# Gate matrices of an expert layer: one-hot tiles interleaved by two tokens instead of four

## The chip, the cores and the metric

The kernel runs on one core of one Trainium2 chip. The core has five engines that run side by side: TensorE (PE; its weight loads are listed apart as PEld), VectorE (DVE), ScalarE (ACT), GpSimd (POOL) and SyncE (SP, which here issues DMAs). The metric is the device time of one execution in microseconds.

## The reference

The program is two blocks of two layers each, on 256 tokens of width 1024. The change lies in the expert part (`peer`) of the first block, which runs once per layer:

```python
s1 = jnp.einsum("thd,hnd->thn", q1, k1); s2 = jnp.einsum("thd,hnd->thn", q2, k2)
v1, i1 = lax.top_k(s1, TOPK); v2, i2 = lax.top_k(s2, TOPK)       # TOPK 16, 128 keys, 8 heads
cand = (v1[..., :, None] + v2[..., None, :]).reshape(t, PEER_HEADS, TOPK * TOPK)
sv, ci = lax.top_k(cand, TOPK)
e1 = jnp.take_along_axis(i1, ci // TOPK, axis=-1); e2 = jnp.take_along_axis(i2, ci % TOPK, axis=-1)
experts = e1 * N_KEYS + e2                                       # one of 128 x 128
gates = jax.nn.softmax(sv, axis=-1)
hid = jax.nn.gelu(jnp.einsum("td,tkd->tk", xi, u_tab[ei]))
out = jnp.einsum("tk,tkd->td", gi * hid, v_tab[ei])
```

Each token picks 128 pairs (8 heads x 16) of a row key `e1` and a column key `e2`, each with a gate.

## The kernel before

The kernel doesn't gather experts. It computes the hidden values of all 128 x 128 experts for all tokens, multiplies them by a gate matrix that is zero for what wasn't picked, and multiplies by all of `v`. The result of the first two lies in `big`, 128 partitions x 128 x 256 tokens.

The expert rows (`peer`, lines 1109 to 1119): for each `j` of 128 one `gemm` (line 464) with 8 pieces of the width, three matmuls each, since every f32 matrix is split into a high and a low part: 24 matmuls of 128 x 256 into the PSUM tile `mm`. Weights come by DMA into `st` and are split by ScalarE (`wh`) and VectorE (`wl`) in line 381. After each `gemm`, `pump` lets a generator (`topk`) emit some of its instructions, and `hid` (line 1201) applies the gelu and, where the token's gate is there already, multiplies by it (line 1208).

The gates (`topk`, lines 1312 to 1346): after the top-k the tile `egt` holds, for each of 128 picks on the partitions and each token, the row key, the column key, and the gate as two f16 parts. For a block of 4 tokens VectorE makes four f16 tiles of 128 x 512 in one buffer `o` (two buffers, carved out of `x`, so that the trace calls them `x`): `o[:, 0]` and `o[:, 1]` are one where the index equals the row or the column key (line 1324), and `o[:, 2]` and `o[:, 3]` are `o[:, 1]` times the two gate parts (line 1326). Then TensorE makes each token's 128 x 128 gate matrix as two matmuls (line 1346, recorded as line 430, `g<-x`), with `o[:, 0]` as weights and `o[:, 2]`, `o[:, 3]` as the moving operand, for that token alone: 8 matmuls per block, 64 blocks per layer, two layers. VectorE (line 1335) and ScalarE (line 1337) write the gates into `big`.

Within a tile the index is the slow dimension and the token of the block the fast one: element `4 * i + t`. So VectorE's operands have runs of four, and a matmul for token `q` reads every fourth element, a step of 8 bytes. `iota4` is the index row repeated in that layout, cast once per layer (line 1074).

The order in which instructions stand on an engine is set when the program is built, by a list scheduler with a cost model; each engine then works in that order.

Of the kernel before, what the change touches and what calls it, by code (L numbers as in the profile page):

```python
# [12 lines left out]
F16 = mybir.dt.float16  # L13
# [6 lines left out]
P = 128  # L20
# [392 lines left out]
class Builder:  # L413
# [635 lines left out]
    def peer(self, l):  # L1049
        nc, tc = self.nc, self.tc  # L1050
        with tc.tile_pool(name=f"pe{l}", bufs=1) as sp, tc.tile_pool(name=f"pew{l}", bufs=2) as wk, \
                tc.tile_pool(name=f"pep{l}", bufs=2, space=PSUM) as pp:
            big = self.t(sp, [P, P, T], tag="big")
            egt = self.t(sp, [P, 4, T], F16, tag="egt")
            self.big, self.egt = big, egt
            self.iota8 = self.t(sp, [P, 16, 8], F16, tag="iota8")
            self.iota4 = self.t(sp, [P, 4 * P], F16, tag="iota4")
            with tc.tile_pool(name=f"peh{l}", bufs=1) as hp:
                hi = self.t(hp, [P, KD, T], F32R, tag="hi")
                lo = self.t(hp, [P, KD, T], F32R, tag="lo")  # L1060
                flat = big.rearrange("p j t -> p (j t)")
                front = Carve(flat[:, :4096], 4096)
                tail = Carve(flat[:, J0 * T:], (P - J0) * T)
                pk = self.t(tail, [P, 2, 1024], tag="pk", bufs=1)
                for n in range(2):
                    nc.gpsimd.dma_start(pk[:, n], self.I["pk"][l, n])
                self.warm(pp, "g", WP[0], 2)
                ss = self.sumsq((self.t(self.psp, [P, 512], tag="pss", bufs=1) if FD & 1 else self.t(pp, [P, 512], tag="mm"))[:, :T])
                self.warm(pp, "g", WP[1], 2)
                r = self.rsq(ss, T, front, tag="nrm", bufs=1)  # L1070
                self.norm(self.x, lambda k: self.g(f"norm2_g{l}", k), None, hi, lo, front, r)
                with self.after(self.nins):
                    nc.vector.tensor_copy(self.iota8, self.iota[:, :16].unsqueeze(2).to_broadcast([P, 16, 8]))
                    nc.vector.tensor_copy(self.iota4.rearrange("p (i t) -> p i t", t=4),
                                          self.iota.unsqueeze(2).to_broadcast([P, P, 4]))
                nc.gpsimd.dma_start(self.xd[l], self.x)
                self.ohp = Carve(self.x.rearrange("p k t -> p (k t)"), KD * T)
                rhs = lambda k: (hi[:, k, :], lo[:, k, :])
                sc = [self.t(tail, [P, 16, P], tag="sc") for _ in range(2)]
                scp = None  # L1080
                pend = []

                def score(b, ps):
                    nonlocal scp
                    qt = self.t(front, [P, T], tag="qt")
                    nc.scalar.copy(qt, ps)
                    if b % 4 == 0:
                        scp = [self.t(pp, [P, 4, P], tag=f"sc{t}", bufs=1) for t in range(2)]
                    key = pk[:, b % 2, (b // 2) * P:(b // 2 + 1) * P]
                    for t in range(2):  # L1090
                        self.mm(scp[t][:, b % 4, :], qt[:, t * P:(t + 1) * P], key, start=True, stop=True)
                    if b % 4 == 3:
                        for t in range(2):
                            nc.scalar.copy(sc[t][:, b - 3:b + 1, :], scp[t])
                        self.scored = b + 1

                self.J, self.gtok, self.scored = 0, 0, 0
                self.tkdone = False
                self.bg.append(self.topk(l, sc, tail, wk, pp))
                for b in range(16):  # L1100
                    w = self.stream.get("wq", (l, b), 0, 1024)
                    ps = self.t(pp, [P, 512], tag="mm")[:, :T]
                    self.gemm(ps, w, KD, rhs)
                    self.pump(PUMP0)
                    if pend:
                        score(*pend.pop())
                    pend.append((b, ps))
                score(*pend.pop())
                for j in range(P):
                    if j == J0:  # L1110
                        while not self.tkdone:
                            self.pump(1)
                    w = self.stream.get("u", (l, j), 0, 1024)
                    ps = self.t(pp, [P, 512], tag="mm")[:, :T]
                    self.gemm(ps, w, KD, rhs)
                    self.pump(PUMP if j < J0 else PUMP2)
                    if pend:
                        self.hid(*pend.pop(), wk)
                    pend.append((j, ps))
                self.hid(*pend.pop(), wk)  # L1120
                self.drain()
# [3 lines left out]
            with tc.tile_pool(name=f"pev{l}", bufs=2) as vp:  # L1125
# [24 lines left out]
                for j in range(P):  # L1150
# [23 lines left out]
                    for gs in ((0,), (1,), (2,), (3,)) if last else ((0, 2), (1, 3)):  # L1174
                        a = gs[0] % 2
                        ts = slice(a * P, (a + 1) * P)
                        for q, wh, wl, vh, vl in W:
                            for w, vs in ((wh, (vh, vl)), (wl, (vh,))):
                                for g in gs:
                                    h = g // 2  # L1180
                                    for v in vs:
                                        self.mm(acc[g], w[:, q % 2, ts], v[:, h * 512:(h + 1) * 512],
                                                start=q == 0 and w is wh and v is vh,
                                                stop=q == P - 1 and w is wl)
# [28 lines left out]
    def topk(self, l, sc, tl, wk, pp):  # L1213
        nc, big, egt = self.nc, self.big, self.egt
# [21 lines left out]
        for t in range(2):  # L1236
# [22 lines left out]
            g = hk(eg[:, 2, :])  # L1259
# [45 lines left out]
            ps = self.t(pp, [P, 4, P], tag="sc0", bufs=1)  # L1305
# [6 lines left out]
        NB = T // 4  # L1312
        oh = {}
        gp = {}
        io = self.iota4.rearrange("p (i t) -> p i t", t=4)
        for b in range(NB + 2):
            if b < NB:
                o = self.t(self.ohp, [P, 4, 4 * P], F16, tag="oh", bufs=2)
                o = o.rearrange("p n (i t) -> p n i t", t=4)
                oh[b] = o  # L1320
                e = [egt[:, n, 4 * b:4 * b + 4].unsqueeze(1).to_broadcast([P, P, 4]) for n in range(4)]
                for n in range(4):
                    if n < 2:
                        nc.vector.tensor_tensor(o[:, n], io, e[n], op=OP.is_equal)
                    else:
                        nc.vector.tensor_tensor(o[:, n], o[:, 1], e[n], op=OP.mult)  # L1326
                    yield 330
            if b >= 2:
                ps = gp.pop(b - 2)
                t0 = 4 * (b - 2)  # L1330
                J = self.J
                pv = ps.rearrange("p t j -> p j t")
                if J > 0:
                    d = big[:, :J, t0:t0 + 4]
                    nc.vector.scalar_tensor_tensor(d, pv[:, :J, :], 1.0 / GS, d, op0=OP.mult, op1=OP.mult)
                if J < P:
                    nc.scalar.activation(big[:, J:, t0:t0 + 4], pv[:, J:, :], AF.Copy, scale=1.0 / GS)
                self.gtok = t0 + 4
                yield 450
            if 1 <= b <= NB:  # L1340
                o = oh.pop(b - 1)
                ps = self.t(pp, [P, 4, P], tag="g")
                gp[b - 1] = ps
                for q in range(4):
                    for n in range(2, 4):
                        self.mm(ps[:, q, :], o[:, 0, :, q], o[:, n, :, q], start=q == 0 and n == 2, stop=n == 3)

    def mods(self, l, qs, acc, pool):
        nc = self.nc
# [745 lines left out]
```

## Time and profile before

| what | us |
|---|---|
| median of 3 runs (lowest, highest) | 3112.36 (3111.44, 3113.1) |
| profiled execution: time, span | 3113.49, 3111.7 |
| PE busy | 3021.3 |
| DVE busy | 2226.6 |
| ACT busy | 1504.2 |
| POOL busy | 216.9 |

The span runs from the first to the last instruction; the rest of the profiled execution's time lies around it. A busy TensorE is not one at its peak: matmuls are pipelined, their recorded durations overlap, and the pace is read from the distance of their starts. Nearly all of TensorE's matmuls have one line, 430, since a helper records them; the tiles' names tell them apart.

### The profile page before, as it was taken

Reading aid. Unit: us, or ns where it says so; the run is one execution under the profiler, and the core shown is the slowest. Engines: PE = TensorE matmul, PEld = TensorE weight load, DVE = VectorE, ACT = ScalarE, POOL = GpSimd, SP = SyncE. Lnnn points to the kernel's source line nnn. Section 1 sums busy time; section 2 is a strip of 40 time slices with the busy share of each in tenths; the row PEclk is TensorE's granted clock in tenths of the full one; section 3 lists DMA queues with packets and bytes.
Section 4 is the critical chain, followed back from the end, with each engine's and each line's share of the span. In section 5 each row is a group of like instructions: output and inputs, shape, how many; then the busy total and the mean of one; then the engine's idle time right before and its main releaser. Section 6 shows DMA issues by size and latency. Waiting matters only on the chain. (4 is left out here: it accounts for less than half of the span.)

```text
span 3111.7 us, 50024 instructions
## 1 busy us (share of the span) xinstructions
PE 3021.3 (97%) x19130; PEld 2674.5 (86%) x19130; DVE 2226.6 (72%) x4322; ACT 1504.2 (48%) x2547; POOL 216.9 (7%) x262
## 2 busy tenths in 40 slices
PE   7999999999999889999999999998999999999999
PEld 7899999987887879999997788776688878977899
DVE  8789688789555969868869855667567773476554
ACT  7545444444444655444444444557532222377443
POOL 4200000000001720000000000100020001100100
PEclk8999999999999999999999999999999999999999
DMA  4455544578665445654458766521145553231455
GB/s 153 142 160 180 159 140 136 159 267 276 191 193 176 127 138 163 180 153 138 141 164 291 255 190 193 160 73 39 38 135 183 183 180 107 100 102 55 136 183 149
DMA packets 133599, 489.32 MB, mean 157 GB/s; under 512 B 15024, under 2 KB 15280, under 8 KB 132208
## 3 DMA queue, kind: packets, MB, share of 16 engines
q1 hardware_dynamic: 130608, 472.65, 49.2%
q0 software_dynamic: 2608, 13.44, 1.3%
q8 instruction: 150, 2.46, 0.3%
q14 instruction: 89, 0.73, 0.1%
q10 hardware_dynamic: 144, 0.05, 0.0%
HBM read 480.83 MB, written 5.24 MB: 156 GB/s over the span
## 5 line engine op out<-in xcount | busy, mean ns | idle before, releaser
L381 ACT CAST wh<-st 128x1024 fp32r<-128x1024 f32 (+1 forms) x797 | 832.6, 1046 | 1071.6 <-PE mm L430 657.8
L381 DVE TENSOR_TENSOR wl<-st,wh 128x1024 fp32r<-128x1024 f32 (+1 forms) x797 | 975.8, 1226 | 442.7 <-ACT wh L381 439.6
L430 PE MATMUL mm<-hi,wh 128*128 128x256 f32 (+1 forms) x3552 | 1086.9, 308 | 11.7 <-DVE hi L643 8.1
L430 PE MATMUL mm<-hi,wl 128*128 128x256 f32 (+1 forms) x3552 | 1065.7, 300 | 6.7 <-DVE wl L381 6.7
L430 PE MATMUL mm<-lo,wh 128*128 128x256 f32 (+1 forms) x3552 | 1066.8, 301 | 3.1 <-DVE lo L643 2.8
L430 PEld LDWEIGHTS mm<-hi,wh 128*128 128x128 f32 x3552 | 682.6, 193 | 46.6 <-issue 9.3
L430 PEld LDWEIGHTS mm<-lo,wh 128*128 128x128 f32 x3552 | 683.6, 192 | 29.4 <-DVE lo L643 6.8
L430 PEld LDWEIGHTS mm<-hi,wl 128*128 128x128 f32 x3552 | 682.5, 192 | 29.6 <-DVE wl L381 8.0
L430 PE MATMUL sc<-wl,wwh 128*128 128x512 f32 x496 | 195.2, 394 | 0.0
L430 PE MATMUL g<-wl,wwh 128*128 128x512 f32 x496 | 193.2, 389 | 0.0
L430 PE MATMUL g<-wh,wwl 128*128 128x512 f32 x496 | 193.1, 389 | 0.0
L430 PE MATMUL sc<-wh,wwl 128*128 128x512 f32 x496 | 193.1, 389 | 0.0
L430 PE MATMUL sc<-wh,wwh 128*128 128x512 f32 x496 | 192.3, 389 | 0.0
L430 PE MATMUL g<-wh,wwh 128*128 128x512 f32 x496 | 192.3, 389 | 0.0
L1326 DVE TENSOR_TENSOR x<-x,egt 128x512 f16<-128x512 f16 x256 | 107.3, 422 | 84.2 <-PE g L430 84.2
L1155 ACT CAST wwh<-big 128x512 fp32r<-128x512 f32 x124 | 77.2, 624 | 148.0 <-PE g L430 148.0
L430 PE MATMUL g<-x 128*128 128x128 f16 x1024 | 142.5, 296 | 0.0
L1394 DVE SCALAR_TENSOR_TENSOR sreg<-tl,silc,sreg 128x512 f32<-128x512 f32 x168 | 120.0, 747 | 7.3 <-DMA tl<-in_mod 6.9
L1394 DVE SCALAR_TENSOR_TENSOR sreg<-mb,silc,sreg 128x512 f32<-128x512 f32 x168 | 117.0, 747 | 8.7 <-DMA mb<-in_mod 8.4
L430 PE MATMUL mm<-fl,wh 128*128 128x256 f32 (+1 forms) x374 | 122.4, 327 | 0.0
L430 PE MATMUL mm<-fh,wh 128*128 128x256 f32 (+1 forms) x374 | 122.4, 327 | 0.0
L430 PE MATMUL mm<-fh,wl 128*128 128x256 f32 (+1 forms) x374 | 122.3, 327 | 0.0
(551 smaller groups left out, 4376.1 us busy)
## 6 DMA issues: line engine op xcount, KB each, us to landing
st<-in_u SPq DMA_DIRECT2D x256, 512.0 KB, 3.7
st<-in_v SPq DMA_DIRECT2D x256, 512.0 KB, 3.8
st<-in_fi SPq DMA_DIRECT2D x88, 512.0 KB, 3.4
st<-in_w SPq DMA_DIRECT2D x58, 512.0 KB, 3.7
tl<-in_mod SPq DMA_DIRECT2D x48, 512.0 KB, 4.9
mb<-in_mod SPq DMA_DIRECT2D x48, 512.0 KB, 4.3
st<-in_wq SPq DMA_DIRECT2D x32, 512.0 KB, 4.0
st<-in_fo SPq DMA_DIRECT2D x32, 512.0 KB, 3.7
```

The costliest lines, as they stand in the source:

```text
L381: self.last = [b.nc.scalar.copy(hi, t).ins, b.nc.vector.tensor_sub(lo, t, hi).ins]
L430: self.lastmm = self.nc.tensor.matmul(out, lhsT=a, rhs=b, start=start, stop=stop, skip_group_check=True).ins
L1155: nc.scalar.copy(wh, big[:, j:j + 2, :])
L1326: nc.vector.tensor_tensor(o[:, n], o[:, 1], e[n], op=OP.mult)
L1394: nc.vector.scalar_tensor_tensor(a, w[:, k % 2], s, a, op0=OP.mult, op1=OP.add)
```

## The change

The four tokens of a block are laid out as two groups of two: element `256 * g + 2 * i + t`. A matmul for token `q` now reads group `q // 2`, every second element: a step of 4 bytes, for the weights and the moving operand. VectorE's instructions keep their number and size, but the pattern of the operands changes: the key operand has runs of two that are repeated 128 times in each of two groups, and the index row (`iota2`, half as long) is repeated for the two groups. The cast that lays it out has 256 elements a partition in place of 512. On all five engines the instructions stand in the same order as before, one for one.

```diff
@@ peer
-            self.iota4 = self.t(sp, [P, 4 * P], F16, tag="iota4")
+            self.iota2 = self.t(sp, [P, 2 * P], F16, tag="iota2")
...
-                    nc.vector.tensor_copy(self.iota4.rearrange("p (i t) -> p i t", t=4),
-                                          self.iota.unsqueeze(2).to_broadcast([P, P, 4]))
+                    nc.vector.tensor_copy(self.iota2.rearrange("p (i t) -> p i t", t=2),
+                                          self.iota.unsqueeze(2).to_broadcast([P, P, 2]))
@@ topk
-        io = self.iota4.rearrange("p (i t) -> p i t", t=4)
+        io = self.iota2.rearrange("p (i t) -> p i t", t=2).unsqueeze(1).to_broadcast([P, 2, P, 2])
...
-                o = o.rearrange("p n (i t) -> p n i t", t=4)
+                o = o.rearrange("p n (g i t) -> p n g i t", g=2, t=2)
                 oh[b] = o
-                e = [egt[:, n, 4 * b:4 * b + 4].unsqueeze(1).to_broadcast([P, P, 4]) for n in range(4)]
+                e = [egt[:, n, 4 * b:4 * b + 4].rearrange("p (g t) -> p g t", g=2).unsqueeze(2)
+                     .to_broadcast([P, 2, P, 2]) for n in range(4)]
...
-                        self.mm(ps[:, q, :], o[:, 0, :, q], o[:, n, :, q], start=q == 0 and n == 2, stop=n == 3)
+                        self.mm(ps[:, q, :], o[:, 0, q // 2, :, q % 2], o[:, n, q // 2, :, q % 2],
+                                start=q == 0 and n == 2, stop=n == 3)
```

## Rows read from the trace of the kernel before

**Rows 1.** The page: busy time by engine, and the chain that ended last.

```profile
PE 3021.3 (97%) x19130; PEld 2674.5 (86%) x19130; DVE 2226.6 (72%) x4322; ACT 1504.2 (48%) x2547; POOL 216.9 (7%) x262
...
PE mm L430 22%; PE s L430 3%; PE o L430 1%; PE pt L1749 1%; PE pss L430 0%; PE ss L430 0%; DVE lo L643 0%; ACT wh L381 0%; PE pss L1362 0%; DVE mb L643 0%; DVE hi L643 0%; DMA mb<-in_mod 0%; DVE wl L381 0%; DMA st<-in_fi 0%; ACT at L1750 0%
```

**Rows 2.** Stretches: length, busy PE, PEld, DVE, ACT, POOL, clock, DMA share, GB/s.

```profile
372.00:548.00 176.00, 176.00 (x1478) 173.53 (x1477) 144.77 (x324) 80.23 (x185) 0.00 (x0) 1.00 0.46 138
...
586.00:630.00 44.00, 44.00 (x369) 44.00 (x368) 23.41 (x30) 20.74 (x31) 0.00 (x0) 1.00 0.62 181
...
1370.00:1546.00 176.00, 176.00 (x1477) 173.50 (x1476) 144.75 (x322) 80.26 (x185) 0.00 (x0) 1.00 0.46 138
...
525.00:548.00 23.00, 23.00 (x195) 22.68 (x194) 19.93 (x44) 10.13 (x25) 0.00 (x0) 1.00 0.47 137
555.40:563.00 7.60, 7.60 (x66) 7.54 (x64) 7.43 (x17) 3.56 (x10) 0.00 (x0) 1.00 0.45 140
```

**Rows 3.** Groups by shape, 372 to 548 us: busy, mean ns | idle before.

```profile
L430 PEld LDWEIGHTS mm<-hi,wh 128*128 128x128 f32 x368 | 71.0, 193 | 0.1
...
L1324 DVE TENSOR_TENSOR x<-iota,egt 128x512 f16<-128x512 f16 x93 | 38.9, 419 | 0.0
L1326 DVE TENSOR_TENSOR x<-x,egt 128x512 f16<-128x512 f16 x92 | 38.9, 422 | 31.2 <-PE g L430 31.2
L430 PEld LDWEIGHTS <-x 128*128 128x128 f16 x372 | 37.6, 118 | 2.4
```

**Rows 4.** Timeline, from 395 us: start, duration, engine, instruction.

```profile
395.04 1.10 PE L430 MATMUL g<-x 128*128 128x128 f16 x8
...
395.85 0.21 PEld L430 LDWEIGHTS mm<-hi,wh 128*128 128x128 f32 x1
395.90 0.37 PE L430 MATMUL mm<-hi,wh 128*128 128x256 f32 x1
...
398.85 1.12 PE L430 MATMUL g<-x 128*128 128x128 f16 x8
...
402.67 1.11 PE L430 MATMUL g<-x 128*128 128x128 f16 x8
```

**Rows 5.** Timeline of TensorE without gates: the first and the 25th matmul.

```profile
590.04 0.28 PE L430 MATMUL mm<-lo,wh 128*128 128x256 f32 x1
...
592.92 0.28 PE L430 MATMUL mm<-lo,wh 128*128 128x256 f32 x1
```

**Rows 6.** Timeline of bf16 matmuls in the attention of layer 0.

```profile
82.79 0.38 PE L430 MATMUL s<-kt,qz 128*128 128x256 f32 x1
...
83.12 0.22 PE L430 MATMUL s<-maskb,identb 128*128 128x128 bf16 x1
...
83.17 0.22 PE L430 MATMUL s<-cum,oh 128*128 128x128 bf16 x1
83.17 0.10 PEld L430 LDWEIGHTS <-identb 128*128 128x128 bf16 x1
83.23 0.22 PE L430 MATMUL s<-maskb,identb 128*128 128x128 bf16 x1
83.23 0.19 PEld L430 LDWEIGHTS s<-kt,qz 128*128 128x128 f32 x1
83.28 0.43 PE L430 MATMUL s<-kt,qz 128*128 128x256 f32 x1
```

**Rows 7.** Tile `g`: all gate matmuls, ns least/median/most, first and last start.

```profile
L430 PE MATMUL g<-x x1024: 282/297/302, 289.3 to 1577.6; 128*128 128x128 f16 x171
```

**Rows 8.** VectorE: groups of 280 to 340 us, then line 1156.

```profile
L1302 DVE TENSOR_TENSOR big<-big 128x1024 f16<-128x1024 f16 x2 | 1.4, 682 | 0.0
L1296 DVE TENSOR_TENSOR big<-big,iota 128x2048 f16<-128x2048 f16 x1 | 1.2, 1218 | 0.0
L1302 DVE TENSOR_TENSOR big<-big 128x512 f16<-128x512 f16 x2 | 0.8, 395 | 0.0
...
L1156 DVE TENSOR_TENSOR wwl<-big,wwh x124: 677/692/695, 638.5 to 1978.5; 128x512 fp32r<-128x512 f32 x124
```

## The prediction

> **What bounds the kernel now.** I read the page first. TensorE is busy for 97% of the span, VectorE for 72%, and the chain that ended last is made of TensorE's matmuls of line 430 for nearly all that it follows back [rows 1]. So the question for each stage is whether TensorE ever waits in it. I then took the stretches. The gate matmuls of a layer run in one stretch, spread between the hidden-layer matmuls of the expert rows: 372 to 548 us in layer 0 and 1370 to 1546 us in layer 1 hold most of them. [...] Grouped by shape, VectorE's only wait in the first stretch is 31.2 us, of `x` (line 1326) for the gate matmuls, 0.68 us in each of the 46 periods [rows 3]. VectorE waits for TensorE and not the other way, and a us taken off TensorE here is a us off the end, until VectorE's 0.68 us are used up.
>
> Then one period of the stretch in order of time. It holds one expert row of 24 matmuls of 256 columns, and one gate block of 8 matmuls of 128 columns. Blocks start at 395.04, 398.85 and 402.67 us, so a period is 3.82 us [rows 4]. The same 24 matmuls without gates take 2.88 us (from 590.04 to 592.92), 0.120 us each, at the same clock [rows 2, 5]. So a gate block costs 3.82 - 2.88 = 0.94 us, or 0.1175 us per matmul of 128 columns. A matmul of half the columns takes the time of a whole one.
>
> **Why they are slow.** Three rows stand around it. The bf16 matmuls of the attention, 128 columns with no gaps between elements, each with its own weight load, start 0.055 us apart: 83.12, 83.17, 83.23 [rows 6]. That is 0.43 ns a column, against 0.92 ns for the gates. The expert-row matmuls read 256 columns of 4 bytes, 1024 bytes in each partition, in 0.120 us. The gates read 128 columns at a step of 8 bytes, again 1024 bytes of span, in 0.1175 us. [...] The weight load is the other strided operand. It takes 118 ns [rows 3]; the dense bf16 load takes 0.10 us and runs under a spacing of 0.055, and the f32 loads take 193 ns and run under a spacing of 0.120 [rows 3, 5, 6]. A load of 118 ns hence need not hold the matmuls at 0.1175.
>
> [...]
>
> **The change part by part.** The order of instructions is the same on all five engines, one for one; only access patterns differ, and one cast of half the size.
>
> 1. The matmuls. 128 columns at a step of 4 bytes span 512 bytes, so by the pace of the expert rows 0.120 x 512/1024 = 0.060 us. The ends: 0.055 us (dense bf16, the floor), and 0.067 us. The latter comes from reading the 0.120 us as 256 columns at 0.0535 us per 128 plus a fixed 0.013, and keeping the fixed part whole. I take 0.060, the value of the nearest row, which moves the same 4 bytes per column.
>
> 2. The way out of a block. Here not all of the gain is kept. The weights of the next expert row are f32, and their load starts with the last gate matmul. In the bf16 rows the load of `kt` starts at 83.23; the matmul behind it is issued at 83.28 but takes 0.43 us, where the next one like it takes 0.38 (82.79 shows it), so it really begins 0.05 us later than issued, at 83.33, 0.10 us after its load's start. In the gate rows the load starts at 395.85, the matmul is issued at 395.90 and takes 0.37 in place of 0.28, so it begins at 395.99, 0.14 us after its load's start [rows 4 to 6]. A gate matmul of 0.1175 us hides nearly all of that; one of 0.060 doesn't. So the last of eight costs 0.10 to 0.14 us whatever its step; I take 0.12, the middle.
>
> A block then takes 7 x 0.060 + 0.12 = 0.54 us in place of 0.94, which saves 0.40 us. There are 1024 gate matmuls in all, 128 blocks of 8, from 289 to 1578 us [rows 7]: 128 x 0.40 = 51.2 us. With the ends: 7 x 0.055 + 0.10 = 0.485 saves 58 us, and 7 x 0.067 + 0.14 = 0.609 saves 42 us.
>
> 3. The one-hot tiles on VectorE. Four instructions per block, 419 and 422 ns each [rows 3], with as many elements as before, in 16 bit. Their second operand is now read in runs of two elements instead of four. No row here has runs of two. Plain f16 additions (line 1302) take 395 ns for 512 elements and 682 for 1024, so 0.56 ns an element, by which 2048 would take 1256; line 1296, with 2048 in runs of eight, takes 1218 [rows 8]. So runs of eight are free, and today's runs of four cost at most 25 ns over the plain 395. The low end is hence -25 ns. For the high end I take a full loss of the doubled 16-bit rate: an f32 subtraction of 512 elements (line 1156) takes 692 ns, or +270 [rows 8]. I take 0, nearest to the rows of f16, and keep +270 for a rival. What hides it: VectorE needs 3.82 - 0.68 = 3.14 us of a period on average; the new period is 2.88 + 0.54 = 3.42 us. That leaves 0.28 us, or 70 ns for each of the four. VectorE's need grows along the stretch, since line 1335 covers more of `big` each time: at the end its busy time is 19.93 of 23 us, or 3.31 us of a period [rows 2]. So it still fits, by 0.11 us, at the end. Only in the last blocks (555.4 to 563 us, two periods) is VectorE busy for 7.43 of 7.60 us [rows 2], against 6.84 us that TensorE will ask for: up to 0.6 us lost per layer, inside the bounds.
>
> 4. The cast that lays out the index row (line 1074) runs twice in the program and has 256 elements now, not 512. VectorE's 512 elements of line 1324 take 419 ns [rows 3], so this gives back some 0.4 us at most; I cost it at nothing.
>
> 5. What the faster period asks of others. ScalarE is busy for 80.2 of 176 us; the DMA share is 0.46 there, and at 586 to 630 us, where a row takes 2.88 us, it is 0.62 [rows 2]: this supply already runs at a shorter period than the new one. So nothing is late next.
>
> **The sum.** The profiled execution took 3113.5 us (span 3111.7, and 1.8 around it). Less 51.2 it is 3062.3. The median of the runs, 3112.4, lies 1.1 lower; I predict 3061 us. The forecast's own range is 3053 to 3072, from the ends above with 1 to 2 us for run and tail.
>
> **Rivals.**
> *Only part of it.* The pace falls with the step but not to half, say 0.090 us per matmul, between floor and today: a block of 7 x 0.090 + 0.12 = 0.75 us saves 24 us, 3089 us. For it: the moving and the stationary operand are both strided and read at once, and no row here shows this together at 4 bytes in 16 bit. Against: f32 columns at 4 bytes do reach 0.060 us per 128.
>
> *Nothing.* Any gap between 16-bit elements, or something else than the step, sets 0.1175 us. Then TensorE stays as it is, 3112 us. [...] Against: the equality of 1024 bytes in 0.120 and 0.1175 us would be chance.
>
> *Slower: VectorE becomes the bound.* Runs of two elements lose the doubled 16-bit rate, +270 ns on each of four. VectorE then needs 3.14 + 1.08 = 4.22 us a period, more than today's 3.82; TensorE waits for the one-hot tiles in each block, and 128 x 0.40 = 51 us are added: 3163 us. It eats into the gain from 490 ns (3.42 us of need) and makes a loss from 590 ns on (3.82 us). For it: the shortest runs in the trace are of four, and these are 25 ns slower than none. Against: going from eight to four cost no more than that. [...]
>
> **How the numbers follow.** Chances: the forecast 0.73, part of it 0.09, nothing 0.10, slower 0.08. A change under 0.2% (6 us) can't be told from none here. Faster is the first two, 0.82; the same 0.10; slower 0.08. The range for 8 in 10 takes the forecast's bounds, with some us below for a cheaper way out of a block, and the partial case to its weaker part: 3050 to 3100 us.
>
> **What would show it.** In the profile of the changed kernel a period of the stretch should be 3.42 us (3.37 to 3.49), and the first expert-row matmul behind a gate block should wait longer than now, 0.43 us or more in place of 0.37. `x` of lines 1324 and 1326 should stay within 395 to 445 ns, and VectorE's wait for the gate matmuls should shrink from 0.68 to about 0.3 us a period. A period of 3.82 with unchanged `x` would show the step to be innocent. An `x` near 690 ns and TensorE waiting for it would show the slower rival. If the first row behind a block didn't wait longer, step 2 would be wrong, and the gain near 60 us.

## The result and the profile after

The changed kernel takes 3057.74 us (median of 4 runs, 3055.53 to 3061.81) against 3111.9 us before (4 runs, 3109.22 to 3113.1): 0.9831 of the time, 95% interval 0.9817 to 0.9846. That is 54.2 us less, where 51.2 were forecast (3061 us). The profiled execution has a span of 3054.9 us, 56.8 less than before.

The stretches first (columns as in [rows 2]: length, busy PE, PEld, DVE, ACT, POOL, granted clock, DMA share, GB/s). The first line is the even part of layer 0's gates, the second holds its last blocks.

```profile
365.00:524.00 159.00, 159.00 (x1500) 157.02 (x1499) 146.78 (x329) 81.21 (x187) 0.00 (x0) 1.00 0.53 156
...
526.00:549.00 23.00, 22.53 (x212) 22.23 (x210) 22.28 (x47) 9.97 (x26) 0.00 (x0) 1.00 0.49 143
```

TensorE is still busy for all of the even part: it remains the bound, and VectorE has moved from 82% of the stretch to 92%. In the last blocks VectorE is nearly full, and TensorE for the first time is not.

The timeline of one period (start, duration, engine, instruction) answers to [rows 4].

```profile
395.58 0.64 PE L430 MATMUL g<-x 128*128 128x128 f16 x8
...
396.00 0.19 PEld L430 LDWEIGHTS mm<-hi,wh 128*128 128x128 f32 x1
396.02 0.36 PE L430 MATMUL mm<-hi,wh 128*128 128x256 f32 x1
...
398.98 0.64 PE L430 MATMUL g<-x 128*128 128x128 f16 x8
```

A period is 398.98 - 395.58 = 3.40 us in place of 3.82, where 3.42 were forecast. With 2.88 us for the 24 expert-row matmuls, a block takes 0.52 us in place of 0.94. The load behind it starts at 396.00; the matmul is issued at 396.02 and takes 0.36 in place of 0.28, so it begins at 396.10, 0.10 us after its load's start. The last gate matmul, issued at 396.00, therefore costs 0.10 us or a little more, and the seven others (0.52 - 0.10)/7 = 0.060 us each. By the starts of this period in ns it is 0.070 us for the first, 0.057 to 0.061 for the six behind it, and 0.106 for the last.

The groups of 365 to 524 us (busy, mean ns | idle before) answer to [rows 3]. Lines 1325 and 1327 are lines 1324 and 1326 of before.

```profile
L1327 DVE TENSOR_TENSOR x<-x,egt 128x512 f16<-128x512 f16 x94 | 39.7, 423 | 12.2 <-PE g L430 11.2
L1325 DVE TENSOR_TENSOR x<-iota,egt 128x512 f16<-128x512 f16 x94 | 39.3, 418 | 0.0
...
L430 PEld LDWEIGHTS <-x 128*128 128x128 f16 x376 | 21.8, 97 | 2.0
```

VectorE's one-hot instructions take 418 and 423 ns, as before: runs of two cost nothing over runs of four. Its idle time in front of line 1327 is 12.2 us in 47 periods, 0.26 us each, where 0.68 - 0.42 = 0.26 was left. The weight load has fallen too, from 118 ns to 97.

Last, the tile `g` (ns least/median/most, first and last start), which answers to [rows 7].

```profile
L430 PE MATMUL g<-x x1024: 218/218/234, 285.2 to 1521.5; 128*128 128x128 f16 x171
```

From the first to the last gate matmul it is 1236.3 us in place of 1288.3: 52.0 us went here. The first one starts 4.1 us earlier than before. Of that, 2.9 us stood already at 140 us, ahead of any changed instruction, and the first gate matmul is early in `stat4` and `step16` too (285.3 and 286.7 us, against 289.3 before): these executions differ by so much in their first stretch, and this part of the 56.8 us isn't the change's.

### The profile page after: what moved, and what is told of

It is laid out like the page before. It is cut to its first block, busy times and chain, and to the rows that moved or that the text cites. A ratio compares the mean times of both kernels' runs of the same rounds, so it can differ in the third digit from the quotient of the medians.

```text
span 3054.9 us, 50024 instructions
## 1 busy us (share of the span) xinstructions
PE 2960.3 (97%) x19130; PEld 2615.3 (86%) x19130; DVE 2225.5 (73%) x4322; ACT 1502.1 (49%) x2547; POOL 216.1 (7%) x262
## 5 line engine op out<-in xcount | busy, mean ns | idle before, releaser
L1156 DVE TENSOR_TENSOR wwl<-big,wwh 128x512 fp32r<-128x512 f32 x124 | 85.3, 689 | 48.6 <-ACT wwh L1155 48.5
```

Of the source, the lines that this page charges most:

```text
L1156: nc.vector.tensor_sub(wl, big[:, j:j + 2, :], wh)
```

## The experiments

**Which operand sets the pace.** The two tiles of a matmul were given different steps. `mov4` keeps the layout of before for the row key `o[:, 0]`, the weights, and the new one for the rest; `stat4` is the reverse, with `two = (0,)`. (`o[0]` is the view of the buffer in the new layout, `o[1]` that of before; VectorE writes each tile in the layout in which it is read.)

```diff
+        two = (1, 2, 3)
...
-                        self.mm(ps[:, q, :], o[:, 0, q // 2, :, q % 2], o[:, n, q // 2, :, q % 2],
-                                start=q == 0 and n == 2, stop=n == 3)
+                        w, m = (o[0][:, k, q // 2, :, q % 2] if k in two else o[1][:, k, :, q] for k in (0, n))
+                        self.mm(ps[:, q, :], w, m, start=q == 0 and n == 2, stop=n == 3)
```

> Only the moving tiles (the two gate parts, and the column key from which they are made) step by 4 bytes; the row key, the weights, still steps by 8. Theory (the moving operand's step sets the pace, the load is hidden): gate matmuls 0.058 us apart as in the changed kernel, period 3.40 us, 3058 us, though the loads stay near 117 ns. Rival (the strided weight load sets the pace): 0.1175 us, period 3.82 us, 3112 us. Both halves: some 0.09 us, 3085 us.

> The reverse: only the weights step by 4 bytes, the moving tiles still by 8. Theory: loads fall to 97 ns, but the matmuls stay at 0.107 to 0.1175 us, 3105 to 3112 us. Rival (the load sets the pace): 0.058 us, 3058 us.

Measured: `mov4` 3061.27 us, 0.9841 of before (0.9824 to 0.9857); `stat4` 3104.34 us, 0.9978 (0.9969 to 0.9988). Loads and matmuls of `mov4` over the whole program, then two block starts:

```profile
L430 PEld LDWEIGHTS <-x x1024: 112/113/135, 285.4 to 1526.6; 128*128 128x128 f16 x171
L430 PE MATMUL g<-x x1024: 218/221/252, 285.4 to 1526.7; 128*128 128x128 f16 x171
...
420.10 0.66 PE L430 MATMUL g<-x 128*128 128x128 f16 x8
423.52 0.67 PE L430 MATMUL g<-x 128*128 128x128 f16 x8
```

And the same of `stat4`:

```profile
L430 PEld LDWEIGHTS <-x x1024: 96/115/119, 285.3 to 1570.2; 128*128 128x128 f16 x171
L430 PE MATMUL g<-x x1024: 274/296/300, 285.3 to 1570.3; 128*128 128x128 f16 x171
...
421.09 1.09 PE L430 MATMUL g<-x 128*128 128x128 f16 x8
424.88 1.09 PE L430 MATMUL g<-x 128*128 128x128 f16 x8
```

With the moving operand alone at 4 bytes a period is 3.42 us and nine tenths of the gain are there, though its loads take 113 ns. With the weights alone at 4 bytes it is 3.79; the loads, expected at 97 ns, are recorded with 115 there. The rival of the load falls as the main cause. It isn't quite nothing: `stat4` is 5.7 us faster than before (3110.0 us in these runs), by an interval that excludes no change, and a little below its expected range. The two parts, 48.7 and 5.7 us, add up to 54.4. From the first to the last gate matmul, where the edits act, the profiles show less for the weights: 1285.0 us in place of 1288.3, so 3.3, and 47.0 for the moving operand (1241.3).

**The other direction: 16 bytes.** The two tiles of a pair are interleaved too; VectorE's runs are of four.

```diff
+                o = o.rearrange("p n c -> p (n c)").rearrange("p (a i m t) -> p a m i t", a=2, m=2, t=4)
+                o = [o[:, n // 2, n % 2] for n in range(4)]
...
+                        self.mm(ps[:, q, :], o[0][:, :, q], o[n][:, :, q], start=q == 0 and n == 2, stop=n == 3)
```

> The two tiles of a pair are interleaved as well, so that both operands step by 16 bytes; VectorE has runs of four as before the change. Theory (pace follows the bytes walked over): 128 x 16 = 2048 bytes take 0.235 us, a block 1.88 us and a period 4.75 us, 128 x 0.94 = 120 us more than before, 3232 us. Rival (any gap between 16-bit elements costs the same): 3112 us. [...]

Measured: 3240.3 us, 1.0415 of before (1.0394 to 1.0436): 130 us more, where 120 were expected.

```profile
420.41 2.06 PE L430 MATMUL g<-x 128*128 128x128 f16 x8
425.19 2.06 PE L430 MATMUL g<-x 128*128 128x128 f16 x8
```

A period of 4.78 us, 4.75 forecast: the pace does follow the step, in both directions. "Any gap costs the same" falls. The 10 us beyond the forecast weren't traced.

**No gap at all, and what VectorE says to it.**

```diff
+        io = self.iota1.unsqueeze(1).to_broadcast([P, 4, P])
...
+                o = o.rearrange("p n (t i) -> p n t i", t=4)
...
+                e = [egt[:, n, 4 * b:4 * b + 4].unsqueeze(2).to_broadcast([P, 4, P]) for n in range(4)]
...
+                        self.mm(ps[:, q, :], o[:, 0, q, :], o[:, n, q, :], start=q == 0 and n == 2, stop=n == 3)
```

> Each token's column lies without gaps (step of 2 bytes); VectorE's key operand is then one element read 128 times. Theory: gate matmuls at 0.055 us, but VectorE loses the doubled 16-bit rate, 690 ns for each of four in place of 420, needs 4.22 us a period and becomes the bound: 3163 us, with TensorE waiting for x. Rival (VectorE keeps its rate, or has room): 3055 us.

Measured: 3134.44 us, 1.0075 of before (1.0055 to 1.0095). The groups of 372 to 548 us, the stretch itself, and one of its waits (who waited for whom: us in total, times, longest):

```profile
L430 PE MATMUL mm<-hi,wh 128*128 128x256 f32 x348 | 103.2, 297 | 14.7 <-ACT big L498 14.7
...
L1323 DVE TENSOR_TENSOR x<-iota,egt 128x512 f16<-128x512 f16 x86 | 57.8, 679 | 0.0
L1325 DVE TENSOR_TENSOR x<-x,egt 128x512 f16<-128x512 f16 x85 | 55.6, 679 | 0.0
...
372.00:548.00 176.00, 153.94 (x1379) 148.31 (x1379) 176.00 (x300) 74.82 (x172) 0.00 (x0) 0.98 0.43 130
...
ACT gl L498 <- DVE big L1207: 25.3, 25, 2.3
```

This layout brings about the slower rival of the prediction. The one-hot instructions take 679 ns, VectorE is busy for all 176 us, and TensorE now waits for 22 of them. So VectorE has become the bound, as the rival said. The wait stands elsewhere, though: the rival and the expectation have TensorE wait for the one-hot tiles `x`, and it waits at most 1.4 us for those in this stretch. 14.7 us of its idle time lie in front of expert rows, until ScalarE's gelu (line 498) is done, and 5.9 in front of gate matmuls, until ScalarE has written earlier gates (line 1336). ScalarE itself waits 25.3 us for VectorE's multiplication by the gates (line 1207, which is 1208 of before): what comes late is other work of the full VectorE. The price was twice too high, 24.4 us in place of 51. In this stretch 336 gate matmuls, 42 blocks, are done, so a block takes 4.19 us, close to the 4.22 of the rival. But not all 64 blocks of a layer lie in such a stretch: the first ones have two expert rows each to hide behind. The scheduler also laid the gates out otherwise here, and how the rest comes about wasn't traced.

**The disputed cost by itself.** Into the changed kernel, ahead of the first expert layer, series of 24 matmuls were put whose results nobody uses, with f32 matmuls on a constant between them (`g<-ones_d`, recorded as 4 in the first kernel and 60 in the second). `sw` and `sx` are the steps of weights and moving operand in elements.

```diff
+        step = lambda a, s, n=P: a[:, :n * s].rearrange("p (i t) -> p i t", t=s)[:, :, 0]
...
+            for sw, sx in BENCH:
+                for _ in range(24):
+                    mm(step(h, sw), step(h, sx))
+                mark()
```

> The changed kernel with 16 series of 24 matmuls of 128 columns put ahead of the first expert layer, results unused, each series with other steps of weights and moving operand, two f32 matmuls between series. [...] Rival (any gap halves the rate): 4 bytes would be slow here too, or 6 to 16 all alike at 0.11. Rival (weights matter): weights at 8 or 16 bytes with a dense moving operand give 0.1 us or more. Last series: 24 pairs of one f16 matmul of 128 and one f32 matmul of 256 columns; if an f32 load behind a short matmul shows by 0.05 us, a pair takes 0.23 us or more, if it is hidden 0.18 us.

The first six series of `micro`, f16 with both steps at 2, 4, 6, 8, 12 and 16 bytes, and one with the moving operand alone at 8:

```profile
149.91 1.50 PE L433 MATMUL g<-big 128*128 128x128 f16 x24
151.25 0.66 PE L433 MATMUL g<-ones_d 128*128 128x128 f32 x4
151.75 1.54 PE L433 MATMUL g<-big 128*128 128x128 f16 x24
153.12 0.66 PE L433 MATMUL g<-ones_d 128*128 128x128 f32 x4
153.62 2.25 PE L433 MATMUL g<-big 128*128 128x128 f16 x24
155.70 0.64 PE L433 MATMUL g<-ones_d 128*128 128x128 f32 x4
156.17 2.99 PE L433 MATMUL g<-big 128*128 128x128 f16 x24
158.98 0.62 PE L433 MATMUL g<-ones_d 128*128 128x128 f32 x4
159.44 4.33 PE L433 MATMUL g<-big 128*128 128x128 f16 x24
163.59 0.63 PE L433 MATMUL g<-ones_d 128*128 128x128 f32 x4
164.05 5.79 PE L433 MATMUL g<-big 128*128 128x128 f16 x24
169.66 1.03 PE L433 MATMUL g<-ones_d 128*128 128x128 f32 x4
...
180.69 2.94 PE L433 MATMUL g<-big 128*128 128x128 f16 x24
183.46 0.62 PE L433 MATMUL g<-ones_d 128*128 128x128 f32 x4
```

From a series' start to that of what follows, divided by 24:

| step, bytes | 2 | 4 | 6 | 8 | 12 | 16 | 8, moving alone |
|---|---|---|---|---|---|---|---|
| us per matmul | 0.056 | 0.057 | 0.087 | 0.117 | 0.173 | 0.234 | 0.115 |
| bytes walked per ns | 4.6 | 9.0 | 8.8 | 8.8 | 8.9 | 8.8 | 8.9 |

From 4 bytes on the pace is 8.8 to 9.0 bytes of span per ns, and below that a floor of 0.056 us. At 4 bytes both meet (0.057 us), which is why the change gets nearly all that dense columns would give. The granted clock was 1.00 in these series but for the one at 16 bytes, where it was 0.83 (last section); `step16`, at 1.00, bears its pace out, with (4.78 - 2.88)/8 = 0.237 us. At 8 bytes the matmul takes 2.1 times the dense one, at 16 bytes 4.2 times.

The last series alternates one f16 matmul and one f32 matmul of 256 columns; three of the pairs begin at:

```profile
204.01 0.24 PE L433 MATMUL g<-big 128*128 128x128 f16 x1
...
204.25 0.23 PE L433 MATMUL g<-big 128*128 128x128 f16 x1
...
204.50 0.23 PE L433 MATMUL g<-big 128*128 128x128 f16 x1
```

A pair takes 0.245 us, where 0.057 + 0.12 = 0.177 would be its parts: going from a short matmul to an f32 one and back costs 0.07 us. That it is the f32 load is argued: the four f32 matmuls behind a series take 0.66 us after steps of 2 and 4 bytes and 0.62 after 8, as if a longer matmul in front hid more of it. A cost of the change of type wasn't tried apart from it.

The f32 series of 128 columns don't follow the bytes. The one at 4 bytes:

```profile
194.05 2.87 PE L433 MATMUL g<-hi 128*128 128x128 f32 x24
196.76 0.66 PE L433 MATMUL g<-ones_d 128*128 128x128 f32 x4
```

They took 0.113, 0.118 and 0.121 us at 4, 8 and 16 bytes, where 8.8 bytes per ns would give 0.058, 0.116 and 0.233. The clock wasn't read in them, but the four f32 matmuls behind each took 0.63 to 0.66 us, as behind the series at a granted clock of 1.00 (0.62 to 0.66). An f32 matmul of half the columns isn't faster than 0.113, against 0.122 for 256 columns (below), and a step of 16 bytes adds next to nothing. What holds it there wasn't tried.

The weights' steps alone came out as 0.107 us for 8 bytes and 0.072 for 16 there, but at a granted clock of 0.50 and 0.84 (last section), so they were tried again, with f32 beside them.

> As the kernel with the series, with other series and 30 f32 matmuls between them, so that the clock is at its upper level in each. f16, weights at 2, 8 and 16 bytes with a dense moving operand of 128 columns: 0.055 to 0.063 us each if weight steps don't set the pace, 0.1 us and more if they do. f16 with 256 columns, both at 4 bytes, then both at 8: 0.11 and 0.235 us if the pace is per column moved, with nothing per matmul. f32 with 256 columns at 4, 8, 16 bytes: 0.12, 0.235, 0.47 us if f32 follows the bytes walked over as the prediction read its rows; 0.12 for all three if its own rate or its load sets 0.12. f32 with 512 columns at 4 and 8 bytes: 0.227 and 0.47, or 0.227 twice.

Weights at 8 and at 16 bytes with dense columns, then f32 with 256 columns at 4, 8 and 16 bytes:

```profile
157.98 1.50 PE L433 MATMUL g<-big 128*128 128x128 f16 x24
159.32 6.92 PE L433 MATMUL g<-ones_d 128*128 128x128 f32 x60
...
166.08 1.64 PE L433 MATMUL g<-big 128*128 128x128 f16 x24
167.55 6.92 PE L433 MATMUL g<-ones_d 128*128 128x128 f32 x60
...
195.87 3.11 PE L433 MATMUL g<-hi 128*128 128x256 f32 x24
198.81 6.86 PE L433 MATMUL g<-ones_d 128*128 128x128 f32 x60
205.43 5.69 PE L433 MATMUL g<-hi 128*128 128x256 f32 x24
210.94 6.88 PE L433 MATMUL g<-ones_d 128*128 128x128 f32 x60
217.57 5.84 PE L433 MATMUL g<-hi 128*128 128x256 f32 x24
223.23 6.88 PE L433 MATMUL g<-ones_d 128*128 128x128 f32 x60
```

The 60 f32 matmuls behind each series took 6.86 to 6.92 us, so the clock seems to have been the same in all, and a dense f16 series took 0.056 us, as it did in `micro` at a granted clock of 1.00. The weights' step leaves 0.056 us at 8 bytes and 0.061 at 16. For f32 with 256 columns the pace is 0.122, 0.230 and 0.236 us: it doubles from 4 to 8 bytes, as the bytes walked would have it, but does not double again to 16, so neither of the two expected answers held. With 512 columns it was 0.232 and 0.454 us at 4 and 8 bytes, as the bytes would have it. The rule of bytes is shown for 16-bit operands from 4 to 16 bytes, and for f32 with 256 columns or more up to 8 bytes only. f16 with 256 columns took 0.114 and 0.230 us at 4 and 8 bytes, twice the 128, so there is no part per matmul to speak of.

## Why the prediction was right

*The bound and the pace (step 1).* Right. 0.060 us was forecast, and 0.060 comes out of the period. In the series by itself it is 0.057. What it rests on, that half the bytes walked take half the time, is what the series and `step16` show for 16 bits, down to a floor of 0.056 us. The bridge to it was in part luck. It halved an f32 row of 256 columns, and an f32 matmul of 128 columns at 4 bytes takes 0.113 us, not 0.060: the argument that f32 columns "do reach 0.060 us per 128" doesn't hold for a matmul of that size. Nor could that row tell bytes from columns, since at 4 bytes a column the floor (2 x 0.056) and the bytes (1024 at 8.8 per ns) give nearly the same time. For 16 bits the rule is right, which only the experiments show. Its upper end, 0.067 with a fixed 0.013 per matmul, turned out to be empty: f16 has no such part.

*The way out of a block (step 2).* Right in kind and near the low end in size: 0.106 us where 0.12 was taken from 0.10 to 0.14. With 0.106 the forecast would have been 7 x 0.060 + 0.106 = 0.526 us per block, 128 x 0.414 = 53.0 us. This is the mis-sized term. Without the step the sum would have been 128 x (0.94 - 0.48) = 59 us. The sign named for it was wrong, though: the matmul behind a block isn't longer than before (0.36 against 0.37 us), since it is also issued sooner, 0.02 us after its load instead of 0.05. What tells is its real start against its load's.

*VectorE (step 3).* Right: 418 and 423 ns, no cost for runs of two, and 0.26 us a period left of its cover, 0.28 forecast. The last blocks were also seen: from 528 us on TensorE waits once, through ScalarE's gelu behind VectorE.

```profile
528.18 1.10 PE L430 MATMUL g<-x 128*128 128x128 f16 x16
529.74 0.39 PE L430 MATMUL mm<-hi,wh 128*128 128x256 f32 x1 [0.47 <-ACT big L498]
```

The row shows 0.47 us of idle time, and layer 1 has the same once; up to 0.6 per layer had been allowed. So the gates' gain is 53.0 us less about 1 us in two layers: the 52.0 us between the first and the last gate matmul. The rest of the 54.2 lies within what runs differ by.

*The weights.* The prediction counted the load at nothing. `stat4` puts it at 3.3 us between the gate matmuls, 5.7 in the medians of whole runs, of some 54; it wasn't wrong to call the load hidden, but not quite complete.

*The rivals.* "Only part" and "nothing" fell by the series and by `step16`, "slower" by 418 ns; `dense` shows that the last one is real one layout further, at half its price and with TensorE's wait in front of the expert rows.

## What to carry to other kernels

Look at the step of a 16-bit moving operand before its number of columns: here up to 4 bytes were free (0.056 and 0.057 us per matmul at 2 and 4) and from there each byte cost in proportion (0.117 at 8, 0.234 at 16), while the weights' step hardly counted (0.061 at 16). When two engines share a tile, the layout that is best for one may cost the other its rate: with dense columns VectorE's one-hot instructions took 679 ns, and a run of two 16-bit elements, at 418 ns, was enough for both. When a group of short matmuls stands between f32 ones, add what its last one costs beyond the others (here 0.106 us in place of 0.058) to the sum of the columns.

## What the runs showed that was not expected

TensorE's granted clock fell with the two f16 series of `micro` whose moving operand steps by 16 bytes: to 0.83 in the first, 0.50 and 0.84 in the two series behind it, and 0.90 in the second. The four f32 matmuls behind each of the two took 1.03 us; behind the f32 series at 16 bytes, where the clock wasn't read, they took 0.63. The windows of the first of them and of the series behind it (weights at 8 bytes, dense columns):

```profile
164.05:169.60 5.55, 5.55 (x26) 3.53 (x25) 0.00 (x0) 0.00 (x0) 0.00 (x0) 0.83 0.02 3
170.49:173.00 2.51, 2.51 (x25) 2.51 (x24) 0.00 (x0) 0.00 (x0) 0.00 (x0) 0.50 0.00 0
```

TensorE is recorded as busy for all of both, yet the granted clock is 0.83 in the first and 0.50 in the second, and the dense series in it took 0.107 us per matmul, about twice its 0.056. The 16-byte series itself keeps its pace: 0.234 us per matmul, where `step16` has 0.237 at 1.00. In `step16`, where blocks at 16 bytes alternate with f32 rows, the clock stayed at 1.00 from 420 to 520 us.

An f32 moving operand at 16 bytes is no slower than at 8 (0.236 and 0.230 us for 256 columns), while an f16 one is twice as slow (0.234 and 0.117 us for 128). Why the two differ stays open.
